# Meta-token state of gated linear attention in full 128-row matmuls, and its first head pair as one chain beside two projections

## The chip, the cores and the metric

The kernel runs on one core of one Trainium2 chip. A core has a matmul engine (TensorE, PE in the profile; PEld is its weight load), two elementwise engines (VectorE, DVE; ScalarE, ACT), GpSimd (POOL), and queues that start transfers (SP's and POOL's here). Each engine works through its own instructions in order and waits on semaphores for the others. The metric is the time of one execution in device microseconds; a kernel's time is the median of its runs.

## The reference

One decoder layer on 512 tokens and 16 learned meta tokens put ahead of them, width 1024. A normed input `u` goes through one wide projection, whose columns feed two branches: a retention branch (4 heads) and a gated linear attention (GLA, 4 heads, keys of 128, values of 256). Both are gated, projected, merged, projected once more and added to the input. The part around the change is GLA:

```python
log_a = log_sigmoid(glr @ w_gate_up + b_gate) / 16.0        # forget gate, per token, head and key channel
b = cumsum(ac, axis=2); b_last = b[:, :, -1]                 # inside a chunk
q_dec, k_inv, k_end = qc * exp(b), kc * exp(-b), kc * exp(b_last[:, :, None] - b)
intra = einsum(where(mask, einsum(q_dec, k_inv), 0), vc)
def step(state, xs):                                         # over chunks
    inter = einsum('bihd,bhde->bihe', q_n, state)
    state = state * exp(a_n)[..., None] + einsum('bjhd,bjhe->bhde', k_n, v_n)
    return state, inter
```

The meta tokens come first, so what they leave behind is the state with which the first token block begins: the sum over 16 rows of decayed keys times values.

## The kernel before

**Numbers.** Everything is float32. A large projection splits each operand into a rounded half (`hi`, type fp32r) and the rest (`lo`) and runs three fp32r matmuls in place of one (hi·hi, hi·lo, lo·hi). ACT casts the `hi` part and DVE subtracts the `lo` part (`split`, L163). Small products of the attention run in plain f32; the trace shows such a matmul as two instructions ("x2").

**Projections.** `quad` multiplies two column blocks of 256 by both halves of the tokens and of the contraction as a two-by-two block product with seven products in place of eight. Each product is 24 matmuls (L327). Two of its operands are weight sums that POOL's queue adds while it loads (L291); the results leave through `copy` (ACT), `put` and `evac` (DVE mostly). Between its products `quad` yields. In its `wide` form two pairs of PSUM banks serve in turn: the first product's bank is copied by ACT before the third product adds into it, and the second product's bank must have been read before the fourth overwrites it.

**Order.** The program is a set of Python generators. `weave(dense, chain, skip)` takes one step of a projection, then one of a chain, and so on, and lets the rest of the chain run out at the end. That order is the priority; the framework's planner then lays each engine's queue out by planned ready times, so a matmul of a projection may be put between matmuls of a chain. `pin` keeps the products of projections in their order, `after` keeps two instructions of one engine in a given order, `act` and `vec` do so for a list.

**GLA.** Heads go in two pairs, p = 0 and p = 1. `gla_attention(p)` is the chain: per block of 128 tokens `decays` (cumulated logs by matmul: tiles `ge` and `gf`, L933 to L937; exponentials on ACT into `gX`; scaled keys and queries `gK` and `gQ` on DVE, L946 and L947), `scores` (`gc`, L957 to L961) and `values` (`go` and `gsu`, L1006 to L1010, then a norm whose power is on POOL, L1022, and a scaling on ACT, L1025). Ahead of block 0 the meta tokens' state is made: `meta_state` (`gm`, L976 and L977), `meta_state2` (a transpose, `gmt`, L987), `meta_state3` (`gs`, L995). These take operands of 16 rows or 16 columns: `gsm`, `lah` and `lal`, `gkm`, `gkmt`, `gvm`. The logs of a block are split into `lah` and `lal`, one buffer each. After block 3's decays ACT applies eight Silus (L1051) to the gate `sg`.

For p = 0 the gate's projection `gla_g(0)` (tile `gg`, seven products) is woven with the first six steps of the attention; the other four steps follow; then the next pair's query and key projection `gla_qk(1)` (`gqk`) is woven with `gla_output(0)` (gating, L1071, and transposes `got`, L1078); then the value projection `gla_v(1)` alone. For p = 1 the attention is woven with `gla_g(1)` and the projections that follow it.

```python
    weave(gla_g(0), gla_attention(0), skip=1)
    weave(gla_qk(1), gla_output(0))
    drain(gla_v(1))
```

Query and key tiles `gq` and `gk` have one buffer each, which both pairs use. The chain's PSUM tiles share four banks (`pat`), those of the projections another four (`ppt`).

Of the kernel before, what the change touches and what calls it, by code (L numbers as in the profile page):

```python
# [21 lines left out]
F32 = mybir.dt.float32  # L22
F32R = mybir.dt.float32r
I32 = mybir.dt.int32
AF = mybir.ActivationFunctionType
# [3 lines left out]
P = 128  # L29
D = 1024  # L30
T = 512
NM = 16
TT = T + NM
HT = TT // 2
# [3 lines left out]
NTB = T // P  # L38
# [14 lines left out]
def constants():  # L53
    c = {}
    pos = np.concatenate([np.arange(NM, NM + 256), np.arange(HM),
                          np.arange(NM + 256, TT), np.arange(HM, NM)]).astype(np.float32)
    half = P
    inv = (10000.0 ** (-np.arange(half) / half)).astype(np.float32)
    ang = (pos[None, :] * inv[:, None].astype(np.float32)).astype(np.float32)
    c["rope"] = np.stack([np.cos(ang), np.sin(ang)], axis=1).astype(np.float32)  # L60

    j = np.arange(P)[:, None]
    cc = np.arange(T)[None, :]
    jm = np.arange(NM)[:, None]
# [24 lines left out]
    mm = np.arange(NM)  # L89
    c["gsum_meta"] = ((mm[:, None] > mm[None, :]) / 16.0).astype(np.float32)  # L90

    jj, ii = np.arange(P)[:, None], np.arange(P)[None, :]
    mA = (jj < 64) & (ii >= 64)
    mB = (jj // 64 == ii // 64) & (jj % 64 < 32) & (ii % 64 >= 32)
    mD = (jj // 32 == ii // 32) & (jj <= ii)
    c["gmask"] = np.stack([mA, mB, mD], axis=1).astype(np.int32)

    sel = np.zeros((P, P), np.float32)
    for g in range(4):
        for r in range(4):  # L100
# [9 lines left out]
def hybrid_kernel(ctx: ExitStack, tc: tile.TileContext, I, out: bass.AP):  # L110
    nc = tc.nc
# [50 lines left out]
    def split(hi, lo, src):  # L162
        return nc.scalar.copy(hi, src), nc.vector.tensor_sub(lo, src, hi.bitcast(F32))  # L163
# [10 lines left out]
    def act(ins):  # L174
        return queue("act", ins)
# [56 lines left out]
    def run(*gens):  # L232
        for g in gens:
            yield from g
# [284 lines left out]
    g1 = gctx.enter_context(tc.tile_pool(name="g1", bufs=1))  # L519
    la = g1.tile([P, 5, 512], F32, name="la")  # L520
    gsum = g1.tile([P, 640], F32R, name="gsum")
    gsm = g1.tile([NM, NM], F32R, name="gsm")
    gmask = g1.tile([P, 3, P], I32, name="gmask")
    gvm = [g1.tile([NM, 512], F32, tag="gvm", name=f"gvm{p}") for p in range(2)]
    gv = [g1.tile([P, NTB, 512], F32, tag="gv", name=f"gv{p}") for p in range(2)]
    gv0 = gv[0]

# [62 lines left out]

    def meta_v(psm, p):
        ps = meta_rows(psm, f"gvm{p}")
        nc.scalar.activation(gvm[p], ps[:NM], AF.Copy, scale=rt[:NM, NTB:])

    pss = [ppt(f"gv0_p{t}") for t in range(NTB)]
    casts = []
# [124 lines left out]
    for x in pmw:  # L721
# [14 lines left out]

    raws = (gsum[:, :512], xc.tile([P, 2, 256], F32, tag="xc", name="gs_raw").rearrange("p a b -> p (a b)"),
            I["gsum"][:, :512]), (gsum[:, 512:], laf[:, 2304:2432], I["gsum"][:, 512:]), \
        (gsm, fa[:NM, 1809:1809 + NM], I["gsum_meta"])
    for dst, raw, src in raws:  # L740
        nc.sync.dma_start(raw, src)
        nc.gpsimd.tensor_copy(dst, raw)
# [6 lines left out]
    def forget_gates():  # L749
# [9 lines left out]
                vec(nc.vector.scalar_tensor_tensor(g[32:64], pr[32:64, s, c0:c1], onec[32:64],  # L759
                                                   g[32:64].bitcast(F32), op0=ALU.add, op1=ALU.subtract))  # L760
        act(nc.scalar.copy(wzs, wz))
        act(nc.scalar.activation(gvm[0], gvs[:NM], AF.Copy, scale=rt[:NM, NTB:]))
        vec(nc.vector.tensor_sub(wzs[64:96], wz[64:96], wzs[64:96].bitcast(F32)))
        yield

# [62 lines left out]
        for b in (0, 4, 1, 2, 3):  # L828
            act(nc.scalar.activation(es[b], es[b], AF.Ln, bias=one))
            vec(nc.vector.tensor_sub(la[:, b, :], la[:, b, :], es[b]))  # L830
            if b == 4:

                parts["la"] = [gp.tile([P, 256], F32R, tag=f"la{x}", name=f"la{x}00") for x in "hl"]
                qsplit(*parts["la"], la[:, 0, :256])
        values(1)

# [16 lines left out]
                                     scale=(rt, rneg)[n][:, 2 * th + i:2 * th + i + 1])  # L853
        return f

    stb = []
    cnt = [0]
    G = {}

# [17 lines left out]
        yield from products  # L877

    def gla_qk(p):
        q = gp.tile([P, 2, T], F32, tag="gq", name=f"gq{p}")  # L880
        k = gp.tile([P, 2, 2, HT], F32, tag="gk", name=f"gk{p}")
        G["q", p], G["k", p] = q, k

        def evac_q(ps):
            for t in range(2):
                vec(nc.vector.tensor_mul(q[:, t, :].rearrange("p (h c) -> p h c", h=2),
                                         ps[t].rearrange("p (h c) -> p h c", h=2), rb[:, :, :256]))

        def evac_k(th, ps):
            for t in range(2):  # L890
                vec(nc.vector.tensor_mul(k[:, t, th, :], ps[t], rb[:, th, :]))

        def evac(n, th, x, y):
            d, w = (q[:, :, th * 256:(th + 1) * 256], 256) if n else (k[:, :, th, :], HT)
            if y is None:
                for t in range(2):
                    nc.vector.scalar_tensor_tensor(d[:, t], x[t][:, :w], (1.0, -1.0)[n], rb[:, th, :w],
                                                   op0=ALU.mult, op1=ALU.mult)
                return
            for t in range(2):  # L900
                nc.vector.tensor_add(d[:, t], x[t][:, :w], y[:, t, :w])
            nc.vector.scalar_tensor_tensor(d, d, (1.0, -1.0)[n], rb[:, th, :w].unsqueeze(1).to_broadcast([P, 2, w]),
                                           op0=ALU.mult, op1=ALU.mult)

        if p:
            yield from quad((C_GK + p * 256, C_GQ + p * 256), False, f"gqk{p}", evac, wide=True)
            return
        yield from proj_a(C_GQ + p * 256, False, f"gq{p}", evac_q)
        yield from proj_a(C_GK + p * 256, True, f"gk{p}", evac_k)

    def gla_attention(p):
# [3 lines left out]
        S = [None, None]  # L915
        Q, K, TO = {}, {}, {}

        def split_la(b, rows):
            if p == b == 0:
                return parts.pop("la")  # L920
            lh = gp.tile([P, 256], F32R, tag="lah", name=f"lah{p}{b}")
            ll = gp.tile([P, 256], F32R, tag="lal", name=f"lal{p}{b}")
            split(lh[:rows], ll[:rows], la[:rows, b, p * 256:(p + 1) * 256])
            return lh, ll

        def decays(b):
            lah, lal = split_la(b, P)
            for h in range(2):
                n = f"{p}{b}{h}"
                hc = h * P  # L930
# [38 lines left out]
                    nc.scalar.copy(KT[b, h], pc[:, 3 * P:])  # L969

        def meta_state():
            lah, lal = split_la(4, NM)
            for h in range(2):
                hc = h * P
                pm = pat(f"gm{p}{h}")
                nc.tensor.matmul(pm[:, :NM], lah[:NM, hc:hc + P], gsm, start=True, stop=False)  # L976
                nc.tensor.matmul(pm[:, :NM], lal[:NM, hc:hc + P], gsm, start=False, stop=True)  # L977
                km = gp.tile([P, NM], F32, tag="gkm", name=f"gkm{p}{h}", bufs=2)
                nc.scalar.activation(km, pm[:, :NM], AF.Exp)
                km2 = km.rearrange("p (h m) -> p h m", h=2)  # L980
                nc.vector.tensor_mul(km2, km2, k[:, h, :, 256:HT])
                S[h] = km

        def meta_state2():
            for h in range(2):
                pt = pat(f"gmt{p}{h}")
                nc.tensor.transpose(pt[:NM, :P], S[h], ident)  # L987
                kmt = gp.tile([P, P], F32, tag="gkt", name=f"gkmt{p}{h}", bufs=3)[:NM]
                nc.scalar.copy(kmt, pt[:NM, :P])
                S[h] = kmt  # L990

        def meta_state3():
# [48 lines left out]
        yield  # L1041
        values(1)
        scores(2)
        yield
        decays(3)

        sg = G["sg", p]
# [163 lines left out]
    for i in range(4):  # L1211
        stb.append(gp.tile([P, P], F32, name=f"stb{i}"))
        nc.gpsimd.memset(stb[i], 0.0)
    weave(gla_g(0), gla_attention(0), skip=1)
    weave(gla_qk(1), gla_output(0))
    drain(gla_v(1))
    weave(run(gla_g(1), gates_first(), gla_branch()), run(gla_attention(1), gla_sums()))
    gctx.close()
# [430 lines left out]
```

## Time and profile before

| | |
|---|---|
| runs shown | 751.65, 751.62, 750.5 us; median 751.62 us |
| the profiled execution | 750.33 us |
| its span, first to last instruction | 748.6 us |
| PE busy | 738.6 us |
| DVE busy | 607.7 us |
| ACT busy | 450.3 us |
| POOL busy | 137.5 us |
| granted PE clock, mean | 0.999 |

The profiled execution's time is its span and 1.73 us around it. Matmuls overlap in the records (one is some 0.28 us long while the next starts 0.11 us behind it), so PE's busy share doesn't say how densely it works; the chain of waits, which gives to each instruction only the time by which it moved the end, does. The stretch that the change touches runs from 58 us (first `gg` product) to 124 us (last `gqk` product), and for the second head pair from 146 us to 182 us.

### The profile page before, as it was taken

Reading aid. Unit: us, or ns where it says so; the run is one execution under the profiler, and the core shown is the slowest. Engines: PE = TensorE matmul, PEld = TensorE weight load, DVE = VectorE, ACT = ScalarE, POOL = GpSimd, SP = SyncE. Lnnn points to the kernel's source line nnn. Section 1 sums busy time; section 2 is a strip of 40 time slices with the busy share of each in tenths; the row PEclk is TensorE's granted clock in tenths of the full one; section 3 lists DMA queues with packets and bytes.
Section 4 is the critical chain, followed back from the end, with each engine's and each line's share of the span. In section 5 each row is a group of like instructions: output and inputs, shape, how many; then the busy total and the mean of one; then the engine's idle time right before and its main releaser. Section 6 shows DMA issues by size and latency. Waiting matters only on the chain.

```text
span 748.6 us, 14064 instructions
## 1 busy us (share of the span) xinstructions
PE 738.6 (99%) x5595; PEld 691.7 (92%) x5595; DVE 607.7 (81%) x873; ACT 450.3 (60%) x764; POOL 137.5 (18%) x172
## 2 busy tenths in 40 slices
PE   9999999999999999999999999999999999999996
PEld 6799899989999999999989999989999989988996
DVE  6699877679897799888957688967697989775995
ACT  7898584666975466546546555646555656532562
POOL 2111110101221122110520100540011210111142
PEclk9999999999999999999999999999999999999999
DMA  9873521821589972734783652796476356687503
GB/s 298 278 162 77 121 62 53 198 85 58 129 187 280 305 169 87 170 113 141 200 250 115 133 149 96 199 213 163 126 169 136 113 141 197 227 195 206 133 29 113
DMA packets 100138, 117.42 MB, mean 157 GB/s; under 512 B 5732, under 2 KB 90852, under 8 KB 99816
## 3 DMA queue, kind: packets, MB, share of 16 engines
q1 hardware_dynamic: 79896, 88.19, 37.1%
q0 software_dynamic: 19888, 27.79, 20.4%
q8 instruction: 44, 0.72, 0.4%
q10 hardware_dynamic: 288, 0.53, 0.2%
q14 instruction: 22, 0.18, 0.1%
HBM read 104.44 MB, written 11.53 MB: 155 GB/s over the span
## 4 chain that ended last, share of the span: by engine, by line
PE 89%; DVE 7%; issue 2%; ACT 1%; POOL 0%; POOLq 0%; DVEq 0%; ACTq 0%
PE rqk_b L327 6%; PE rv_b L327 6%; PE rg_b L327 5%; PE rqk_c L327 5%; PE br_p L201 4%; PE br_p L202 4%; PE br_p L198 4%; PE gg_b L327 3%; PE mg_b L327 3%; PE mr_b L327 3%; PE gv_p L652 3%; PE rv_c L327 3%; PE bg_b L327 2%; PE rg_c L327 2%; PE gk_p L437 2%
## 5 line engine op out<-in xcount | busy, mean ns | idle before, releaser
L202 PE MATMUL br_p<-oh,br_l 128*128 128x512 f32 x128 | 49.9, 390 | 0.0
L201 PE MATMUL br_p<-ol,br_h 128*128 128x512 f32 x128 | 49.9, 390 | 0.0
L198 PE MATMUL br_p<-oh,br_h 128*128 128x512 f32 x128 | 49.8, 389 | 0.0
L163 ACT CAST rv_h<-rv_w 128x1024 fp32r<-128x1024 f32 x24 | 25.3, 1053 | 25.3 <-DVE rv_w L381 10.4
L327 PE MATMUL rqk_b<-xh,rqk_h 128*128 128x264 f32 (+1 forms) x128 | 36.2, 283 | 0.0
L327 PE MATMUL rqk_b<-xh,rqk_l 128*128 128x264 f32 (+1 forms) x128 | 36.1, 282 | 0.0
L327 PE MATMUL rqk_b<-xl,rqk_h 128*128 128x264 f32 (+1 forms) x128 | 36.0, 281 | 0.0
L327 PE MATMUL rv_b<-rv_l,xh 128*128 128x256 f32 x128 | 35.5, 277 | 0.5 <-DVE rv_l L163 0.5
L163 DVE TENSOR_TENSOR rv_l<-rv_w,rv_h 128x1024 fp32r<-128x1024 f32 x24 | 29.3, 1221 | 8.1 <-ACT rv_h L163 8.1
L327 PE MATMUL rv_b<-rv_h,xh 128*128 128x256 f32 x128 | 35.8, 280 | 0.0
L327 PE MATMUL rv_b<-rv_h,xl 128*128 128x256 f32 x128 | 35.4, 277 | 0.0
L327 PE MATMUL rg_b<-rg_h,xh 128*128 128x256 f32 x128 | 35.4, 277 | 0.0
L327 PE MATMUL rg_b<-rg_h,xl 128*128 128x256 f32 x128 | 35.4, 276 | 0.0
L327 PE MATMUL rg_b<-rg_l,xh 128*128 128x256 f32 x128 | 35.4, 276 | 0.0
L163 DVE TENSOR_TENSOR rg_l<-rg_w,rg_h 128x1024 fp32r<-128x1024 f32 x20 | 24.4, 1220 | 8.1 <-ACT rg_h L163 8.1
L163 ACT CAST rg_h<-rg_w 128x1024 fp32r<-128x1024 f32 x20 | 21.0, 1052 | 15.6 <-PE br_p L201 5.9
L291 POOL DMA_DIRECT2D rqk_x<-in_w_in_dram x8 | 10.4, 1302 | 102.2 <-PE rv_b L327 64.2
L202 PEld LDWEIGHTS br_p<-oh,br_l 128*128 128x128 f32 x128 | 24.0, 188 | 5.0
L1380 ACT ACTIVATE on<-av,nm,g_r 128x512 f32<-128x512 f32 x16 | 12.5, 779 | 26.4 <-DVE nm L1378 26.4
L198 PEld LDWEIGHTS br_p<-oh,br_h 128*128 128x128 f32 x128 | 24.0, 188 | 4.6
L201 PEld LDWEIGHTS br_p<-ol,br_h 128*128 128x128 f32 x128 | 24.0, 188 | 4.5
L163 ACT CAST rqk_h<-rqk_w 128x1024 fp32r<-128x1024 f32 x20 | 21.0, 1052 | 11.8 <-PE rqk_c L327 2.9
(624 smaller groups left out, 3155.4 us busy)
## 6 DMA issues: line engine op xcount, KB each, us to landing
rv_w<-in_w_in_dram SPq DMA_DIRECT2D x16, 512.0 KB, 4.2
br_w<-in_w_branch_ret_dram SPq DMA_DIRECT2D x16, 512.0 KB, 3.4
rqk_w<-in_w_in_dram SPq DMA_DIRECT2D x12, 512.0 KB, 5.0
rg_w<-in_w_in_dram SPq DMA_DIRECT2D x12, 512.0 KB, 4.9
rqk_x<-in_w_in_dram SPq DMA_DIRECT2D x8, 512.0 KB, 4.6
rqk_x<-in_w_in_dram POOLq DMA_DIRECT2D x8, 512.0 KB, 7.9
rg_x<-in_w_in_dram SPq DMA_DIRECT2D x8, 512.0 KB, 3.6
rg_x<-in_w_in_dram POOLq DMA_DIRECT2D x8, 512.0 KB, 7.6
```

The lines of the kernel that those rows point to most:

```text
L163: return nc.scalar.copy(hi, src), nc.vector.tensor_sub(lo, src, hi.bitcast(F32))
L198: m = nc.tensor.matmul(o, lh, rh, start=first, stop=False)
L201: nc.tensor.matmul(o, lh, rl, start=False, stop=False)
L202: m = nc.tensor.matmul(o, ll, rh, start=False, stop=last)
L291: x = nc.gpsimd.dma_start(t, block(0, 1), accum_op=ALU.add)
L327: m = nc.tensor.matmul(ps[t][:, :n] if wide else ps[t], l, r, start=first and j == 0, stop=kk == 3 and j == 2, skip_group_check=not fresh ...
L437: m = nc.tensor.matmul(pss[t][th], l[:, kk, c], r, start=first and j == 0, stop=kh == 1 and kk == 3 and j == 2, skip_group_check=not meta ...
L652: m = nc.tensor.matmul(pss[t], (al if j == 1 else ah)[t // 2, kh][:, k, c], (lo if j == 2 else hi)[:, kk, :], start=q == kk == j == 0, sto ...
L1380: nc.scalar.activation(on, ps, AF.Identity, scale=r, bias=nm)
```

## The change

Five edits.

- The constant `gsum_meta` is padded from 16 to 128 rows of zeros; `gsm`, `gvm` and the split of the meta block's logs have 128 rows; the decayed meta keys lie in the first 16 columns of two zeroed 128 x 128 tiles `kms`, used by both head pairs. So `gm`, `gmt` and `gs` are matmuls with 128 rows and 128 weight columns.
- `lah` and `lal` have two buffers.
- For p = 0 one yield goes: `values(1)`, `scores(2)`, `decays(3)` and the Silus are one step.
- `gla_output(0)` follows the attention in one chain, and `gla_qk(1)` follows `gla_g(0)` in one row of projections; the two are woven.
- `gla_qk(1)` takes its `gq` and `gk` tiles only after its first product, when the chain step with `decays(3)` has been written down.

```diff
-    c["gsum_meta"] = ((mm[:, None] > mm[None, :]) / 16.0).astype(np.float32)
+    c["gsum_meta"] = np.concatenate([(mm[:, None] > mm[None, :]) / 16.0, np.zeros((P - NM, NM))]).astype(np.float32)
...
-    gsm = g1.tile([NM, NM], F32R, name="gsm")
+    gsm = g1.tile([P, NM], F32R, name="gsm")
...
-    gvm = [g1.tile([NM, 512], F32, tag="gvm", name=f"gvm{p}") for p in range(2)]
+    gvm = [g1.tile([P, 512], F32, tag="gvm", name=f"gvm{p}") for p in range(2)]
...
-        nc.scalar.activation(gvm[p], ps[:NM], AF.Copy, scale=rt[:NM, NTB:])
+        nc.scalar.activation(gvm[p], ps, AF.Copy, scale=rt[:, NTB:])
...
-        (gsm, fa[:NM, 1809:1809 + NM], I["gsum_meta"])
+        (gsm, fa[:, 1809:1809 + NM], I["gsum_meta"])
...
         if p:
-            yield from quad((C_GK + p * 256, C_GQ + p * 256), False, f"gqk{p}", evac, wide=True)
+            products = quad((C_GK + p * 256, C_GQ + p * 256), False, f"gqk{p}", evac, wide=True)
+            next(products)
+            yield
+            q, k = tiles()
+            yield from products
             return
...
-            lh = gp.tile([P, 256], F32R, tag="lah", name=f"lah{p}{b}")
-            ll = gp.tile([P, 256], F32R, tag="lal", name=f"lal{p}{b}")
-            split(lh[:rows], ll[:rows], la[:rows, b, p * 256:(p + 1) * 256])
+            lh = gp.tile([P, 256], F32R, tag="lah", name=f"lah{p}{b}", bufs=2)
+            ll = gp.tile([P, 256], F32R, tag="lal", name=f"lal{p}{b}", bufs=2)
+            split(lh, ll, la[:, b, p * 256:(p + 1) * 256])
...
-                nc.tensor.matmul(pm[:, :NM], lah[:NM, hc:hc + P], gsm, start=True, stop=False)
-                nc.tensor.matmul(pm[:, :NM], lal[:NM, hc:hc + P], gsm, start=False, stop=True)
-                km = gp.tile([P, NM], F32, tag="gkm", name=f"gkm{p}{h}", bufs=2)
-                nc.scalar.activation(km, pm[:, :NM], AF.Exp)
-                km2 = km.rearrange("p (h m) -> p h m", h=2)
+                nc.tensor.matmul(pm[:, :NM], lah[:, hc:hc + P], gsm, start=True, stop=False)
+                nc.tensor.matmul(pm[:, :NM], lal[:, hc:hc + P], gsm, start=False, stop=True)
+                nc.scalar.activation(kms[h][:, :NM], pm[:, :NM], AF.Exp)
+                km2 = kms[h][:, :NM].rearrange("p (h m) -> p h m", h=2)
                 nc.vector.tensor_mul(km2, km2, k[:, h, :, 256:HT])
-                S[h] = km
...
-                nc.tensor.transpose(pt[:NM, :P], S[h], ident)
-                kmt = gp.tile([P, P], F32, tag="gkt", name=f"gkmt{p}{h}", bufs=3)[:NM]
-                nc.scalar.copy(kmt, pt[:NM, :P])
+                nc.tensor.transpose(pt[:, :P], kms[h], ident)
+                kmt = gp.tile([P, P], F32, tag="gkt", name=f"gkmt{p}{h}", bufs=3)
+                nc.scalar.copy(kmt, pt[:, :P])
...
         scores(2)
-        yield
+        if p:
+            yield
         decays(3)
...
-    weave(gla_g(0), gla_attention(0), skip=1)
-    weave(gla_qk(1), gla_output(0))
+    for h in range(2):
+        kms.append(gp.tile([P, P], F32, name=f"gkm{h}"))
+        nc.gpsimd.memset(kms[h], 0.0)
+    weave(run(gla_g(0), gla_qk(1)), run(gla_attention(0), gla_output(0)), skip=1)
```

More of the change, by code (lines that the diff above doesn't have):

```diff
@@ L761, in forget_gates @@
         act(nc.scalar.copy(wzs, wz))
-        act(nc.scalar.activation(gvm[0], gvs[:NM], AF.Copy, scale=rt[:NM, NTB:]))
+        act(nc.scalar.activation(gvm[0], gvs, AF.Copy, scale=rt[:, NTB:]))
         vec(nc.vector.tensor_sub(wzs[64:96], wz[64:96], wzs[64:96].bitcast(F32)))
@@ L831, in forget_gates @@
             if b == 4:
-                parts["la"] = [gp.tile([P, 256], F32R, tag=f"la{x}", name=f"la{x}00") for x in "hl"]
+                parts["la"] = [gp.tile([P, 256], F32R, tag=f"la{x}", name=f"la{x}00", bufs=2) for x in "hl"]
                 qsplit(*parts["la"], la[:, 0, :256])
@@ L854, in rows_into @@
         return f
-    stb = []
+    stb, kms = [], []
     cnt = [0]
@@ L879, in gla_qk, with tiles @@
     def gla_qk(p):
-        q = gp.tile([P, 2, T], F32, tag="gq", name=f"gq{p}")
-        k = gp.tile([P, 2, 2, HT], F32, tag="gk", name=f"gk{p}")
-        G["q", p], G["k", p] = q, k
+        def tiles():
+            q = gp.tile([P, 2, T], F32, tag="gq", name=f"gq{p}")
+            k = gp.tile([P, 2, 2, HT], F32, tag="gk", name=f"gk{p}")
+            G["q", p], G["k", p] = q, k
+            return q, k
         def evac_q(ps):
@@ L905, in gla_qk @@
         if p:
-            yield from quad((C_GK + p * 256, C_GQ + p * 256), False, f"gqk{p}", evac, wide=True)
+            products = quad((C_GK + p * 256, C_GQ + p * 256), False, f"gqk{p}", evac, wide=True)
[3 more added lines that the diff above has]
+            yield from products
             return
+        q, k = tiles()
         yield from proj_a(C_GQ + p * 256, False, f"gq{p}", evac_q)
@@ L916, in gla_attention, with split_la @@
         Q, K, TO = {}, {}, {}
-        def split_la(b, rows):
+        def split_la(b):
             if p == b == 0:
                 return parts.pop("la")
-            lh = gp.tile([P, 256], F32R, tag="lah", name=f"lah{p}{b}")
-            ll = gp.tile([P, 256], F32R, tag="lal", name=f"lal{p}{b}")
-            split(lh[:rows], ll[:rows], la[:rows, b, p * 256:(p + 1) * 256])
+            lh = gp.tile([P, 256], F32R, tag="lah", name=f"lah{p}{b}", bufs=2)
+            ll = gp.tile([P, 256], F32R, tag="lal", name=f"lal{p}{b}", bufs=2)
+            split(lh, ll, la[:, b, p * 256:(p + 1) * 256])
             return lh, ll
         def decays(b):
-            lah, lal = split_la(b, P)
+            lah, lal = split_la(b)
             for h in range(2):
@@ L971, in meta_state @@
         def meta_state():
-            lah, lal = split_la(4, NM)
+            lah, lal = split_la(4)
             for h in range(2):
```

## The prediction

> **What bounds the kernel now.** First the page: the span, and the chain that ended last, by engine.
>
> ```profile
> span 748.6 us, 14064 instructions
> ...
> PE 89%; DVE 7%; issue 2%; ACT 1%; POOL 0%; POOLq 0%; DVEq 0%; ACTq 0%
> ```
>
> PE carries 89% of the chain, so a microsecond taken from PE's stream is a microsecond of the kernel unless something else is late there. PE's busy share can't say how densely it works, since records overlap. So I went next to busy time by stretch, from the first `gg` product to the last `gqk` product.
>
> ```profile
> core 0: us, PE busy (x) PEld busy (x) DVE busy (x) ACT busy (x) POOL busy (x), PEclk, DMA share, GB/s
> ...
> 64.00:70.00 6.00, 5.99 (x46) 5.44 (x45) 5.86 (x11) 5.65 (x15) 1.69 (x3) 1.00 0.28 87
> ...
> 90.00:97.00 7.00, 6.54 (x39) 5.76 (x39) 6.39 (x15) 5.42 (x17) 1.40 (x4) 1.00 0.04 7
> ```
>
> Only 90 to 97 us shows PE idle, 7.00 - 6.54 = 0.46 us. From 64 to 70 us DVE is nearly full (5.86 of 6.00): a second bound to keep in mind. Transfers are light there (a DMA share of 0.28 and 0.04) and the granted clock is 1.00. What is left to win is thus the price of single matmuls. The chain of waits, in order of time, gives it (start, us by which the piece moved the end, what).
>
> ```profile
> 67.84 0.31 PE gm L976 x2
> 68.16 0.32 PE gg_c L327
> 68.48 0.22 PE gc L957 x2
> ...
> 68.92 0.31 PE gm L977 x2
> 69.23 0.42 PE gc L959 x2
> ...
> 70.43 0.11 PE gc L961
> ...
> 73.17 0.22 PE gmt L987 x2
> 73.39 2.75 PE gg_b L327 x24
> ...
> 78.38 0.62 PE gs L995 x2
> 79.00 0.67 PE gg_c L327 x4
> 79.68 0.62 PE gs L995 x2
> 80.30 1.72 PE gg_c L327 x13
> ...
> 83.22 0.43 PE gsu L1010 x2
> ```
>
> A `gg` matmul costs 2.75 / 24 = 0.115 us in a run of its own kind, but the first one behind `gm` cost 0.32. The pair of `gs` with 16 rows cost 0.62; the pair of `gsu`, the same 256 columns with 128 rows, 0.43. So matmuls of 16 rows cost more than full ones, and so does what stands behind them. The second head pair shows the same:
>
> ```profile
> 152.50 0.23 ACT lah L163
> ...
> 152.77 0.38 PE gm L976 x2
> 153.16 2.36 PE gg_b L327 x19
> 155.52 0.31 PE gm L977 x2
> 155.83 0.79 PE gg_b L327 x5
> ...
> 162.89 0.62 PE gs L995 x2
> 163.51 0.66 PE gg_b L327 x4
> 164.18 0.62 PE gs L995 x2
> 164.80 2.14 PE gg_b L327 x17
> ```
>
> **Part 1: 128 rows.** Sums go by the chain's pieces.
>
> `gm`, first pair: the four matmuls cost 0.31 + 0.31; the matmul behind the first two cost 0.32 - 0.115 = 0.21 too much, the two behind the others 0.42 - 0.22 = 0.20. Together 1.03 us. Second pair: 0.38 + 0.31, then 2.36 - 19 x 0.115 = 0.18 and 0.79 - 5 x 0.115 = 0.22: 1.09 us. Afterwards four fp32r matmuls of 128 rows and 16 columns stand there, a form that the trace doesn't have. At most each costs what `gg` with 256 columns does, 0.115; a cost below zero is excluded, since it still is an instruction with a weight load. I take 0.08, nearer to the record of 128 columns (0.11 for `gc`) than to zero: 0.32 for four. Gain 0.71 and 0.77, with bounds of 0.57 to 1.03 and 0.63 to 1.09.
>
> The Trainium skill ("TensorE: Matmul & The Clock Gate", section "Back-to-back issue gap") puts an issue floor of about 25 ns under matmuls of 1 to 64 columns; by it the four would cost 0.10 and each gain would be 0.22 larger. No run so far shows it.
>
> `gs`, first pair: 0.62 + 0.62, then 0.67 - 4 x 0.115 = 0.21 and 1.72 - 13 x 0.115 = 0.23: 1.68. Afterwards it has `gsu`'s form, 0.43 for each pair of records: 0.86. Gain 0.82. Second pair: 1.24 + 0.20 + 0.19 = 1.63, gain 0.77.
>
> The transposes `gmt` cost 0.22 for two; full ones (`gc` L961) 0.11 each. Nothing.
>
> Rows together: 0.71 + 0.77 + 0.82 + 0.77 = 3.07 us, bounds 2.8 to 3.7.
>
> The same page of the Trainium skill (section "Why this matters for your kernels") says that one matmul with 32 contracted rows takes as long as one with 128, and recommends packing several small ones. By that, padding would win nothing here. The rows above disagree (0.62 against 0.43); it comes back as a rival.
>
> What the padding adds off PE: two zero fills on POOL and a wider cast of `gsm`.
>
> ```profile
> L1213 POOL MEMSET stb<- 128x128 f32 x4 | 0.6, 198 | 0.0
> ...
> L742 POOL CAST gsm<-fg_a 16x16 fp32r<-16x16 f32 x1 | 0.2, 186 | 0.0
> ```
>
> ```profile
> 17.95 0.34 POOL L588 CAST sel<-la 128x128 fp32r<-128x128 f32 x1 [13.45 <-DMA la<-in_sel_dram]
> ...
> 78.53 1.30 POOL L291 DMA_DIRECT2D gqk_x<-in_w_in_dram  x1 [8.31 <-ACT gX L939]
> ```
>
> The fills have the form of `stb`'s, 2 x 0.198 = 0.4 us; POOL then idles 13.45 us before the cast of `sel`, which hides them. Without that cover they cost 0.4. The cast goes from 0.186 to less than the 0.34 of `sel`'s eight times as many columns, and `gm` reads the result only at 67.84. The constant's transfer carries 112 more rows of 64 bytes, with the same one issue on SP. ACT's and DVE's steps on 128 in place of 16 rows keep their row length. All nothing.
>
> **Part 2: one chain beside two projections.** The stall that it can remove: its two ends in the chain of waits, then PE's own record of the second.
>
> ```profile
> 92.47 0.02 issue
> ...
> 95.34 0.45 PE gf L936
> ```
>
> ```profile
> 95.34 0.45 PE L936 MATMUL gf<-gsum,lah 128*128 128x384 f32 x1 [0.46 <-ACT gon L1025]
> ```
>
> `gf` of block 3 needs a PSUM bank that `go` of block 1 holds until its norm (ACT, DVE, POOL, ACT again) is through. From 92.47 to 95.34 the end waits 2.87 us for that. In this time PE did `scores(2)`, six pairs of `gc` at 0.22 and two transposes at 0.11 (1.54 us), and one pair of `ge`, 256 columns as `gg` has (0.23). So PE lost at most 2.87 - 1.54 - 0.23 = 1.10 us, and at least the idle 0.46. Now a whole `gqk` product (24 matmuls as in `gg`'s, some 2.75 us) stands ahead of that step and the next one is ready, with five more to put between the later steps. The planner already pulls single `gqk` matmuls into such gaps, so something of this is lost again where PE's fixed order and ACT's real times disagree. I take 0.8 us, between 0 and 1.10. Less than zero is the slower rival's.
>
> Passed queues: the transfers of `gqk` were issued long before (POOL's second weight sum at 78.53, above), ahead of the steps that move, so neither SP's nor POOL's order changes there. The norm's POOL power keeps its place in the chain. Waits that are added: the second product's evacuation on DVE writes `gk`, which must wait for block 3's `gK` and `gQ`; behind it in DVE's order are only later evacuations and splits, and PE needs that bank at the fourth product.
>
> **Part 3: two buffers for the logs.** The one place where the chain shows the split is the second pair's 152.50: 0.23 us in which PE waits for ACT's cast, which stands behind the exponentials. A second buffer lets it go first: 0 to 0.23 (nothing below, since the later split of a block has no other user to delay), I take 0.1.
>
> **Taken back.** After 67.8 us DVE may not follow. `gg_l` for the fifth product was made at 71.57 and used at 73.35:
>
> ```profile
> 71.57 1.22 DVE L163 TENSOR_TENSOR gg_l<-gg_x,gg_h 128x1024 fp32r<-128x1024 f32 x1
> ```
>
> ```profile
> 73.35 0.28 PE L327 MATMUL gg_b<-gg_l,xh 128*128 128x256 f32 x1
> ```
>
> It ended at 72.79, 0.56 us ahead of its use; PE comes 0.71 earlier, so 0.15 us is lost there, up to 0.5 if the rest of `gm`'s bound is won as well. I take 0.2.
>
> **Sum.** 3.07 + 0.8 + 0.1 - 0.2 = 3.8 us less. Against the profiled execution (750.33 us, span 748.6): 746.5, span 744.8. The median of the runs shown is 1.29 above the profiled execution; there it makes 751.62 - 3.8 = 747.8 us. Nothing behind the changed part takes it back: PE leads the chain there too, and the second pair's steps all start earlier by the same time.
>
> **Rivals.**
>
> *The ACT block comes between the products (slower).* ACT loads a table and runs eight Silus behind block 3's exponentials:
>
> ```profile
> 98.02 1.28 ACT L1051 ACT_TABLE_LOAD   x1
> ...
> 102.28 0.49 ACT L1051 ACTIVATE gsg<-gsg,rneg 128x256 f32<-128x256 f32 x1
> ...
> 103.39 0.36 ACT L340 COPY gqk_x<-gqk_b 128x264 f32<-128x264 f32 x1
> 106.31 1.09 ACT L163 CAST gqk_h<-gqk_x 128x1024 fp32r<-128x1024 f32 x1
> ```
>
> That is 4.75 us, and here the copies of the first `gqk` bank already come after it. The third product adds into that bank and so waits for two copies (0.72); with one cast (1.09) behind the block, 6.6 us of ACT stand before it, and if the chain's own PE steps are stuck behind ACT too, only the second product (2.75) covers. A wait of 3.8, and 1.1 for the next cast: 4.9. Then part 2 gives nothing and 751.6 - 3.07 - 0.1 + 0.2 + 4.9 = 753.5 us. It turns slower from a wait of 3 us on. For it: the copy at 103.39 stands right behind the Silus now. Against: the first bank is now full before block 3's exponentials, where ACT has 7.00 - 5.42 = 1.58 us free, so its copies should go first; and `values(2)` and `scores(3)` need only what stands ahead of the Silus.
>
> *DVE is the bound of the first stretch.* Then the first pair's 1.53 us of rows ends in waits for `lo` parts, and half of part 2 with them: 3.8 - 1.53 - 0.4 = 1.9 less if all else holds, 749.7; with the second pair's `gm` (0.77) lost too, 750.5. For it: 5.86 of 6.00. Against: 6.39 of 7.00 later, and 0.56 us of slack at the split above.
>
> *Rows are not the price.* If the extra is that of a change between fp32r and plain f32, padding wins nothing, and parts 2 and 3 alone remain: 750.7 us. Against it: `gc` is f32 behind fp32r at 68.48 and costs its 0.22; `gm` is fp32r ahead of fp32r at 152.77, and the `gg` behind it still pays. This is also what the Trainium skill's rule on 32 rows (same page and section as above) would make of the time.
>
> *The projection was in the gaps anyway,* so part 2 is nothing: 748.6. This lies inside the forecast's range.
>
> **How the numbers follow.** The forecast (3.8 less, with bounds from 2.8 - 0.5 = 2.3 to 3.7 + 1.1 + 0.2 = 5.0, part 2 at nothing included): 0.70. DVE bound: 0.11. Rows not the price: 0.06. ACT block: 0.08. Another shift of the later plan, either way: 0.05. A measurement of this kernel tells no less than about 0.2%, 1.5 us, from no change. Faster by more: the forecast, a third of the DVE case, half the last: 0.76. Within: the rest of the DVE case, rows not the price, a little of the others: 0.15. Slower: the ACT case and a little: 0.09. The range runs from 751.6 - 5.0 - 0.9 = 745.7 (0.9 for the spread of 1.15 us among the runs shown) to 750.7, where rival three lies; the ACT case and outliers stay outside.
>
> **What would show it.** In the profile after: `gm` and `gs` as 128-row forms, `gs` pairs at 0.43 in the chain and no matmul far above 0.115 behind them; no ACT or POOL piece in the chain between the last `gg` and the first `gqk` product; the last `gqk` product ending some 2 us earlier, `gla_g(1)`'s last some 3.5 us earlier, and that lead kept to the end. It is wrong if `gs` keeps 0.62, if DVE pieces appear in the chain before 90 us, or if `gqk` waits for ACT copies.

## The result and the profile after

The changed kernel takes 749.2 us (median of 12 runs, 748.46 to 750.24), the kernel before beside it 751.0 us (12 runs, 749.9 to 752.43): a ratio of 0.9976 with a 95% interval of 0.9968 to 0.9984. That is 1.8 us less, where 3.8 were forecast. A second timing gave 749.31 against 750.95 us, 0.9977 (0.9968 to 0.9986); one of its 15 runs of the kernel before, 811.63 us at a granted clock of 0.851, was in a slow state and is left out of that ratio (the median without it is 750.85). The profiled execution took 748.96 us, with a span of 747.2.

First the page of the changed kernel: the span and the chain that ended last, by engine.

```profile
span 747.2 us, 14063 instructions
...
PE 83%; DVE 9%; issue 3%; DMA 2%; ACT 2%; POOL 0%; POOLq 0%; DVEq 0%; ACTq 0%
```

PE's share of the chain fell from 89% to 83%, DVE's rose from 7% to 9% and DMA's from 0 to 2%: the end now goes through transfers and elementwise steps in places where PE led before. Busy time by stretch (PE, PEld, DVE, ACT, POOL, granted clock, DMA share, GB/s):

```profile
64.00:70.00 6.00, 5.86 (x51) 5.63 (x50) 6.00 (x11) 5.88 (x15) 4.05 (x3) 1.00 0.28 87
90.00:97.00 7.00, 6.07 (x43) 5.56 (x41) 6.73 (x15) 4.46 (x12) 0.69 (x1) 1.00 0.42 128
```

PE idles 0.93 us between 90 and 97 us, where before it idled 0.46: the stall that the new order was to remove has grown. DVE is full from 64 to 70 us. Then the chain of waits through the first pair:

```profile
64.52 0.14 issue
64.67 0.25 PE gm L983
64.91 0.11 PE gm L984
65.03 2.73 PE gg_b L327 x23
67.76 0.01 PE gm L983
67.77 0.11 PE gm L984
67.88 0.22 PE gg_c L327
...
77.93 0.54 PE gs L1000 x2
78.47 0.48 PE gg_c L327 x4
78.95 0.58 PE gs L1000 x2
79.53 1.16 PE gg_c L327 x10
```

`gs` costs 0.54 and 0.58 where it cost 0.62, and the products behind it nothing extra any more: 0.48 for four and 1.16 for ten are the 0.115 each of a run of their own kind. The first `gm` comes 3 us earlier, and the end is moved by 0.14 us of "issue" just ahead of it. The chain names no releaser. ACT's exponential `gX` ended 0.10 us before (64.30 + 0.27), so a wait for the PSUM bank that it read is likely, but not shown.

Where a part of the extra cost of 16 rows sat can be read from the records of the weight load, before and after:

```profile
78.31 0.29 PEld L995 LDWEIGHTS gs<-gvm,gkmt 16*128 16x128 f32 x2 [0.25 <-ACT gX L940]
78.93 0.19 PEld L327 LDWEIGHTS gg_c<-gg_l,xh 128*128 128x128 f32 x1 [0.33 <-issue]
```

```profile
77.77 0.30 PEld L1000 LDWEIGHTS gs<-gvm,gkmt 128*128 128x128 f32 x2
78.10 0.19 PEld L327 LDWEIGHTS gg_c<-gg_l,xh 128*128 128x128 f32 x1
```

Behind the 16-row `gs` the next weight load began only 0.33 us after the last had ended, together with its own matmul (78.94). Behind the 128-row `gs` it begins 0.03 us after.

Where the time went shows best as a lead. I matched each matmul of two traces with itself and took the difference of the starts, the median in each stretch, less what the traces differ by before any edited code (45 to 58 us: between -0.53 and +0.60 us from execution to execution, already there behind the warm-up matmuls). In us ahead of the kernel before; a minus is behind. The last column is what the `bg` stage takes (221-227 less 235-250).

| kernel | 78-90 | 124-130 | 157-165 | 172-180 | 221-227 | 235-250 | end | lost at `bg` |
|---|---|---|---|---|---|---|---|---|
| changed | 0.89 | 1.10 | 1.85 | 1.65 | 1.79 | 1.00 | 0.93 | 0.79 |
| changed, second profile | 0.89 | 1.09 | 1.84 | 1.05 | 1.18 | 1.15 | 1.09 | 0.03 |
| rows only | 1.17 | 1.17 | 1.52 | 0.89 | 0.89 | -0.21 | -0.22 | 1.10 |
| order only | -0.02 | 0.19 | 0.17 | 0.17 | 0.18 | -0.03 | 0.01 | 0.21 |
| buffers only | -0.01 | -2.49 | -2.02 | -2.18 | -2.07 | -3.24 | -3.29 | 1.17 |
| rows and order | 1.16 | 1.37 | 1.71 | 1.76 | 1.74 | 0.29 | 0.19 | 1.45 |
| second product first | 0.89 | 2.28 | 3.05 | 2.81 | 2.92 | 2.23 | 2.21 | 0.69 |
| `mr` sum later | 0.89 | 1.10 | 1.85 | 2.34 | 2.34 | 0.83 | 0.79 | 1.51 |
| `og` transfer first | 0.89 | 1.10 | 1.85 | 1.28 | 1.40 | 1.39 | 0.87 | 0.01 |
| both of these | 0.87 | 1.05 | 1.80 | 2.29 | 2.29 | 2.19 | 2.17 | 0.10 |
| all three | 0.85 | 2.24 | 3.02 | 3.53 | 3.51 | 3.41 | 3.34 | 0.10 |
| all three, one buffer | 1.15 | 2.54 | 2.91 | 3.31 | 3.41 | 3.41 | 3.36 | 0.00 |

The profiled executions of the changed kernel and of before differ by 0.93 us at the end and by 0.43 in the start, 1.37 us in their times; the medians by 1.8, since the profiled execution of before was a good one (750.33 against its median of 751.0). All leads are against this one execution, so a part of what a kernel seems to lose may be its good luck: its transfer into `og` (below) took 8.2 us, the shortest of the nine profiles that issue it in that order (8.2 to 9.4).

The lead grows to 1.10 us behind the last `gqk` product and to 2.37 just ahead of the second pair's `go` (the row for 164.96 us in the match). Then it is lost in two places. The first is DVE's queue at 160 us, and PE's wait for it:

```profile
160.56 1.23 DVE L364 TENSOR_TENSOR mr_x<-mr_w,mr_w 128x1024 f32<-128x1024 f32 x1 [1.85 <-issue]
...
164.11 0.75 DVE L1002 COPY gS<-gs 128x256 f32<-128x256 f32 x2
```

```profile
164.58 0.70 PE L1011 MATMUL go<-gS,gQ 128*128 128x256 f32 x2 [0.41 <-DVE gS L1002]
```

A weight sum of the `mr` projection waits 1.85 us for its transfer, with the second pair's `gK`, `gQ` and `gS` behind it. It waited as long before (1.90), but PE came later. In the two profiles of the changed kernel this place takes 0.72 and 1.32 us of the 2.37, and the 0.60 between them is the difference of that one transfer (4.4 and 5.0 us). The second is the `bg` stage, in the chain of waits:

```profile
208.43 5.80 DMA bg_x<-in_w_branch_gla_dram
...
214.87 0.80 POOL bg_x L291
215.68 8.29 DMA og<-og1gq
...
224.15 1.07 ACT gs L1157
...
225.24 1.24 DVE gs L1158
...
226.52 5.50 PE bg_b L327 x44
```

A load, the accumulating load behind it on POOL's queue, a transfer into `og` that POOL issues only then, an ACT and a DVE step: PE waits for the last of them.

### The profile page after: what moved, and what is told of

It reads as the page before. It is cut to its first block, busy times and chain, and to the rows that moved or that the text cites. A ratio compares the mean times of both kernels' runs of the same rounds, so it can differ in the third digit from the quotient of the medians.

```text
span 747.2 us, 14063 instructions
## 1 busy us (share of the span) xinstructions
PE 735.6 (98%) x5595; PEld 691.4 (93%) x5595; DVE 607.2 (81%) x873; ACT 450.0 (60%) x764; POOL 140.7 (19%) x174
## 4 chain that ended last, share of the span: by engine, by line
PE 83%; DVE 9%; issue 3%; DMA 2%; ACT 2%; POOL 0%; POOLq 0%; DVEq 0%; ACTq 0%
PE rqk_b L327 6%; PE rv_b L327 6%; PE rg_b L327 5%; PE rqk_c L327 5%; PE br_p L202 4%; PE br_p L201 4%; PE br_p L198 4%; PE gv_p L652 3%; PE mg_b L327 3%; PE rv_c L327 3%; PE rg_c L327 2%; PE mr_b L327 2%; PE gg_b L327 2%; PE bg_b L327 2%; PE gk_p L437 2%
```

## The experiments

All times stand beside the kernel before on the same chip. The ratio and its interval are those of the record and can differ a little from the quotient of the medians. For rows alone, order alone, buffers alone and the second product first, before took 751.0 us (27 runs).

**Rows alone.** Before with the 128-row meta state (the edits to `gsum_meta`, `gsm`, `gvm` and `kms`), in the old order and with one buffer for the logs.

```diff
-                km = gp.tile([P, NM], F32, tag="gkm", name=f"gkm{p}{h}", bufs=2)
+                nc.scalar.activation(kms[h][:, :NM], pm[:, :NM], AF.Exp)
```

> Before with the 128-row meta state alone. Theory A (rows carry the whole gain; the rest of the change gives nothing): 1.5 to 2.0 us faster than before, pairs of gs at 0.54 to 0.58 in the chain in place of 0.62, nothing extra on the gg matmuls behind them. Rival B (the rows' gain of 1.7 us on PE is eaten by waits in both pairs and the woven order carries what is left): under 0.8 us faster.

Measured: 749.77 us, 0.9983 (0.9974 to 0.9992). That is 1.2 us less, between the theory's 1.5 and the rival's 0.8. Its chain of waits through the first pair:

```profile
68.31 0.12 PE gm L976 x2
68.43 0.22 PE gg_c L327
...
69.09 0.12 PE gm L977 x2
69.22 0.32 PE gc L959 x2
...
78.27 0.47 PE gs L993 x2
78.73 0.47 PE gg_c L327 x4
79.20 0.59 PE gs L993 x2
79.79 1.50 PE gg_c L327 x13
```

`gm`: 0.12 + 0.12, and 0.10 too much in each of the pieces behind it: 0.44 in place of 1.03. `gs`: 0.47 + 0.59 and nothing behind: 1.06 in place of 1.68. Together 1.21 us, and the lead table has 1.17. The rows are a price, then: the same matmuls with the same columns got cheaper, and so did what follows them. The second pair wins 0.94 (from 1.17 to 2.11 at 164.96 us). In this execution, the slowest of its 11 (751.04 us), that and more is lost at the `go` wait and in the `bg` stage. (The Trainium skill, "TensorE: Matmul & The Clock Gate", section "Why this matters for your kernels", has a matmul of 32 contracted rows take as long as one of 128; here the pair of 16 rows took 0.62 and that of 128 rows 0.47 to 0.59, and 0.2 less behind it. The measurement decides.)

**Order alone.** The woven chain, the missing yield and the later tiles; 16 rows and one buffer.

```diff
-    weave(gla_g(0), gla_attention(0), skip=1)
-    weave(gla_qk(1), gla_output(0))
+    weave(run(gla_g(0), gla_qk(1)), run(gla_attention(0), gla_output(0)), skip=1)
```

> Before with the woven order alone (attention and output of the first pair as one chain beside gg and gqk, one yield fewer). Theory A: no difference within 0.5 us; gf of block 3 still waits for the bank that go of block 1 holds, PE idle there 0.5 to 1.0 us. Rival B: 0.8 to 1.2 us faster, no idle there.

Measured: 750.39 us, 0.9994 (0.9985 to 1.0003). The lead behind the last `gqk` product is 0.19 us and is gone behind `bg`. PE's stretch around the old stall is emptier than before (3.54 busy of 4.00 there):

```profile
94.00:98.00 4.00, 3.07 (x23) 2.74 (x22) 3.61 (x10) 1.89 (x8) 0.70 (x1) 1.00 0.72 219
```

**Buffers alone.** Before with `bufs=2` on the split logarithms.

```diff
-            lh = gp.tile([P, 256], F32R, tag="lah", name=f"lah{p}{b}")
+            lh = gp.tile([P, 256], F32R, tag="lah", name=f"lah{p}{b}", bufs=2)
```

> Before with two buffers for the split logarithms alone. Theory A: no difference within 0.4 us; gm stands earlier in PE's order and waits about 0.3 us for a PSUM bank that an exponential on ACT still reads. Rival B: 0.2 to 0.5 us faster through the second pair's cast.

Measured: 751.81 us, 1.0010 (1.0002 to 1.0019): slower by 0.8 us. The profiled execution, at 753.36 us the slowest of its 11, shows how the loss grows. POOL's power in the norm took twice its 0.80 us, PE stood, and then ran at half speed (PE's record, POOL's, and busy time by stretch):

```profile
95.93 0.39 PE L933 MATMUL ge<-gsum,lah 128*128 128x256 f32 x1 [1.69 <-ACT gon L1025]
```

```profile
93.40 1.60 POOL L1022 TENSOR_TENSOR gss<-gss,mhalf 128x2 f32<-128x2 f32 x1 [2.49 <-DVE gss L1021]
```

```profile
94.00:98.00 4.00, 2.31 (x16) 1.95 (x14) 2.20 (x9) 2.08 (x7) 1.19 (x2) 0.93 0.45 131
98.00:101.00 3.00, 3.00 (x11) 2.59 (x10) 2.42 (x4) 2.46 (x7) 0.36 (x1) 0.52 0.01 3
```

The granted clock is 0.52 from 98 to 101 us, behind an idle of 1.69 us. The median lost less than this execution, so not every one has it. What the median's 0.8 us are made of isn't settled; the 0.44 us that are lost at the first `gm` (64 to 70 us) are made up by 84.

**Rows and order, one buffer.** The changed kernel without `bufs=2`. For this, the `mr` sum later, the `og` transfer first and all three with two buffers, before took 751.25 us (16 runs).

```diff
-            lh = gp.tile([P, 256], F32R, tag="lah", name=f"lah{p}{b}", bufs=2)
+            lh = gp.tile([P, 256], F32R, tag="lah", name=f"lah{p}{b}")
```

> The changed kernel with one buffer for the split logarithms, as before: rows and order alone. Theory from the run with two buffers alone (0.8 us slower than before): the second buffer lets the first pair's `gm` move ahead to where its PSUM bank is still being read, and PE waits there 0.3 us; without it that wait goes and the kernel is 0.3 to 0.8 us faster than the changed one: about 748.7. Rival: what the two buffers cost alone came from a stall of PE at 94 to 96 us and the lower granted clock (0.52) behind it, which the woven order does not have; then one buffer or two make no difference here (749.2), or one is slower by the 0.23 us that the second pair's cast waited before (749.4).

Measured: 749.73 us, 0.9974 (0.9963 to 0.9985), where the changed kernel has 0.9976: no difference. The profile has both halves: 0.27 more lead at 78 to 90 us without the second buffer, 0.14 less at 157 to 165. The rival's "no difference" held. Its reason, that alone the buffers hurt through the stall at 94 us and the slower clock behind it, is shown by one execution only.

**Second product first.** The changed kernel, with `gqk`'s second product ahead of block 3's decays in the order.

```diff
             next(products)
             yield
+            next(products)
+            yield
             q, k = tiles()
+            next(products)
...
-        if p:
-            yield
+        yield
         decays(3)
```

(`quad` yields once more, ahead of the first write to the tiles.)

> The changed kernel, but with gqk's second product ahead of block 3's decays on PE (a yield more in the projection before its second bank is read, and the attention's yield back). Theory A (the stall at gf is a wait for the PSUM bank of go, which the planner put too early, and nothing else): idle at gf gone, last gqk product 0.8 to 1.2 us earlier than in the changed kernel, 0.5 to 1.0 us faster than it, 2.3 to 2.8 us faster than before. Rival C (PE waits there for ACT's general lateness): the wait moves to the next gqk product, no difference from the changed kernel.

Measured: 748.13 us, 0.9964 (0.9952 to 0.9977). PE's idle time at the old stall is gone (3.07 busy of 4.00 in the changed kernel):

```profile
94.00:98.00 4.00, 4.00 (x36) 3.97 (x35) 2.75 (x10) 1.96 (x8) 0.69 (x1) 1.00 0.87 250
```

The lead behind the last `gqk` product is 2.28 us, 1.18 more than in the changed kernel. So the gain was there, at the place named, and the change didn't fetch it. In the changed kernel PE's record shows why:

```profile
95.75 0.28 PE L941 MATMUL ge<-gsum,lal 128*128 128x256 f32 x1
96.96 0.45 PE L943 MATMUL gf<-gsum,lah 128*128 128x384 f32 x1 [0.93 <-ACT gon L1030]
97.25 0.33 PE L944 MATMUL gf<-gsum,lal 128*128 128x384 f32 x1
97.42 0.28 PE L327 MATMUL gqk_c<-xh,gqk_h 128*128 128x264 f32 x1
```

The first `gqk` product ran ahead of block 1's `go`, so the norm that frees the bank came later too (ACT's `gon` at 96.07, before 94.45), and the second product was queued behind the waiting `gf`. Some 0.4 us of it is DVE's: the norm's `gss` could start when ACT was through at 94.68, but stood behind two `gS` until 95.10.

**`mr` sum later.** The changed kernel, with the waiting weight sum ordered behind `gQ` of block 1.

```diff
-            nc.vector.tensor_add(x3, w22, w12)
+            s = nc.vector.tensor_add(x3, w22, w12)
+            if add_after is not None:
+                after(s, add_after)
```

> The changed kernel, with one of DVE's weight sums (`mr_x`, which waited 1.85 us for its transfer at 160.56 in the changed kernel's profile, with the second pair's gK, gQ and gS of block 1 queued behind it) ordered behind gQ of block 1. Theory: this queueing is what made `go` of block 1 late and cost PE 0.57 us at 164.58; without it the last `mr` product ends 0.4 to 0.6 us earlier. The total follows only as far as the transfer into `og` behind it allows: 0 to 0.5 us faster than the changed kernel, 748.7 to 749.2. Rival: the sum made later delays the first `mr` product in turn, and the last `mr` product ends where it did or later: 749.2 to 749.7.

Measured: 748.29 us, 0.9954 (0.9936 to 0.9971). The `go` wait is gone: PE's record of the same `go` has no idle time,

```profile
165.03 0.59 PE L1013 MATMUL go<-gS,gQ 128*128 128x256 f32 x2
```

and the lead is 2.34 us, where the changed kernel has 1.65 and 1.05. The median lies below the expected 748.7 to 749.2. In the profiled execution, the slowest of its six (750.14 us), the `bg` stage took 1.51 of the lead back, with the longest transfer seen:

```profile
og<-og1gq POOLq DMA_DIRECT2D x1, 512.0 KB, 9.4
```

**`og` transfer first.** The changed kernel, with POOL's issue of the transfer into `og` ahead of the accumulating load of the second `bg` block (called the weight sum in the expectation).

```diff
+                    if t is x3 and behind3 is not None:
+                        after(x, behind3)
...
-        nc.gpsimd.dma_start(a00, a01, accum_op=ALU.add)
+        G["og"] = nc.gpsimd.dma_start(a00, a01, accum_op=ALU.add)
```

> The changed kernel, with one swap in POOL's order: the accumulating transfer into `og` (issued at 215.68 us in the changed kernel's profile, behind the weight sum of the second `bg` block, which itself waited until 214.87 for a load) is issued ahead of that sum. PE, DVE and ACT keep their orders. Theory: this transfer (8.29 us) and the ACT and DVE steps behind it set when `bg_b` at 226.52 can start, so whatever the first stretch wins beyond that point is lost there (PE lost 0.7 us to it). Then the issue moves to about 214, the wait of 0.7 us goes, and the kernel is 0.4 to 0.9 us faster than the changed one: about 748.5. Rival: the transfer waits for its own source instead (the same queue or the same producer), is issued as late as now or takes longer beside the load it passes, or the sum that is now later holds up the `bg` product: no difference (749.2) or slower (749.8).

Measured: 748.98 us, 0.9960 (0.9945 to 0.9975): not told apart from the changed kernel. The `bg` stage took nothing (0.01), as expected, but in this execution the `go` wait had already taken 1.11 (a lead of 2.39 became 1.28, with 0.79 of idle time at that `go`), and at 282 us 0.5 went in the next projection.

**Both of these.** For this, the changed kernel again and all three with one buffer, before took 750.95 us (15 runs).

```diff
+        yield from quad((C_MR, C_MR + 256), False, "mr0", evac, adds=False, add_after=G["gQ", 1, 1])
...
+                            behind3=G["og"] if j else None)
```

> The changed kernel with the `mr` weight sum behind gQ of block 1 and the transfer into `og` ahead of the second `bg` block's accumulating load, without the edit of the `gqk` order. Theory: the 2.3 us of lead that the first of the two edits showed ahead of the `bg` stage is kept through it, so the kernel ends 1.2 to 1.6 us ahead of the changed one, at a ratio of about 0.9957 to before. Rival: the loads and transfers of the `bg` stage cap the lead at about 1.4 us whatever their order (so far the `og` edit alone kept 1.4 behind `bg`): ratio 0.997.

Measured: 748.24 us, 0.9966 (0.9953 to 0.9978), against 749.31 of the changed kernel beside it: 1.07 us. The expected 0.9957 lies inside the interval and so does the rival's 0.997; the profile speaks for the first, since 2.19 of 2.29 us of lead pass the stage. That both edits are needed rests on the profiles: by their ratios one alone (0.9954, 0.9960) and both (0.9966) aren't told apart. Its DMA view has the two transfers that changed places:

```profile
og<-og1gq POOLq DMA_DIRECT2D x1, 512.0 KB, 6.0
...
bg_x<-in_w_branch_gla_dram POOLq DMA_DIRECT2D x1, 512.0 KB, 9.3
```

The transfer into `og` took 5.5 to 6.5 us in the four profiles that issue it first, and 8.2 to 9.4 in the nine that issue it behind the load; PE waits for this one alone.

**The changed kernel again.** The same instructions, beside these.

> The changed kernel once more, every instruction the same, timed beside the kernels that follow. Theory: 1.8 us under the kernel before, as the first time (ratio 0.9976). In its profile the lead over before behind the last `gqk` product is 1.1 us less the difference at the start, and the `bg` stage takes back between 0.2 and 1.5 us of it, by how long the transfer into `og` (8.2 to 9.4 us in the profiles so far) happens to take; if the lead at the end is 0.9 us whatever this transfer takes, that reading falls.

Measured: 749.31 us, 0.9977 (0.9968 to 0.9986). Here the `bg` stage took only 0.03, where the `go` wait had already taken 1.32 of the lead (PE idled 1.01 us there). In these two executions what the first place leaves, the second takes, and the lead at the end is 0.93 and 1.09. My reading that the transfer's length alone decides falls for this pair (8.3 us in both): what counts is the lead with which PE arrives, too. But the loss doesn't need a lead. The kernel with the buffers alone arrives 2.07 us behind and loses 1.17 more, of which 0.9 is its longer transfer (9.1 us against 8.2 before); in rows only the transfer took 9.0 us (a loss of 1.10), in rows and order 9.2 (1.45), in `mr` sum later 9.4 (1.51), so there too most of the loss is its length.

**All three, with two buffers and with one.** The last two edits and the `gqk` order together; then the same without `bufs=2`.

> The changed kernel with all three edits: the second `gqk` product ahead of block 3's decays (1.1 us faster than the changed kernel by itself), the transfer into `og` ahead of the second `bg` block's weight sum, and the `mr` weight sum behind gQ of block 1. Theory: with the transfer issued earlier, the lead that the first stretch wins is kept to the end: the first edit's lead of 3.4 us at the end of the `mr` products (it kept 2.65 behind `bg`) then shows in full, 747.0 to 747.6, and with the `mr` edit 746.7 to 747.4. Rival: behind `bg` another transfer or DVE step is late by as much, and it ends at the first edit's 748.1.

> All three edits, with one buffer for the split logarithms in place of two. Theory: the second buffer costs 0.3 us ahead of 70 us (PE waits for the bank of the first `gm`) and wins about 0.3 at 150 to 165 us, so no difference: 0.9938 of before, as with two. Rival: with the later losses mended the 0.8 us that the second buffer cost alone show: 0.993 or less. Other rival: the second pair's cast waits again and it is 0.3 us slower, 0.9942.

Measured: 747.11 us, 0.9938 (0.9922 to 0.9953), and 746.73 us, 0.9946 (0.9934 to 0.9959). The lead is kept from 157 us to the end, 3.34 and 3.36 us. One buffer or two is no difference. This is 2.1 us under the changed kernel's 749.2 and 2.6 under the 749.31 that was measured beside the second. It is also about what the forecast had promised for the change, by coincidence: two of the three edits are at places that the forecast took at nothing.

## Why the prediction was right in direction and wrong in size

The direction, the range and the place of the first gain held; half of the size was missing. Of the 3.8 us forecast, the lead at 165 us shows 2.37: 2.11 by rows, 0.19 by order, the rest with the buffers. By the forecast's own steps:

- **Part 1, `gs` and `gm` (3.07).** Right mechanism, mis-sized. First pair 1.17 in place of 1.53, second 0.94 in place of 1.54, by rows alone: 2.11, below the lower bound of 2.8. This term was too big by 0.96, more than any other. "Afterwards it has `gsu`'s form, 0.43 for each pair" failed: `gs` took 0.47 to 0.59. That `gs` stands behind fp32r matmuls isn't the reason, since a pair of `go` right behind fp32r `gg_b` costs 0.43 in the same trace (81.03). What differs is the weight load: in the changed kernel that of `gs` starts with its matmul (78.83 both; the pair costs 0.58), that of `go` 0.11 us ahead (80.76 and 80.87); in rows alone that of the first `gs` starts 0.07 ahead (78.03 and 78.10), and the pair costs 0.47. Why it starts late stays open. The `gm` matmuls came out at 0.06 each, below the 0.08 taken, but the piece behind each pair still pays 0.10, taken at zero. The floor of 25 ns for `gm` (the Trainium skill, "TensorE: Matmul & The Clock Gate", section "Back-to-back issue gap") wasn't reached; the same row has about 62 ns per matmul with hardware decode off, which the 0.06 would fit, but no run here shows which of the two holds.
- **Part 2, one chain (0.8).** The step that failed is "Now a whole `gqk` product (24 matmuls as in `gg`'s, some 2.75 us) stands ahead of that step and the next one is ready". It stood ahead of the step that frees the bank as well, and the next one was put behind the wait. Order alone won 0.19. The stall was real: with the second product moved it gave 1.18 more. The mechanism was right, the placing was not read. The bound of 1.10 was wrong twice: PE's `gsu` ran until 92.72, 0.25 us into the wait, which leaves 0.85; and with the second product moved the order wins 1.39 from the row 78-90 to 124-130 (0.89 to 2.28), so more than this stall was to be had there. What the rest is, isn't settled.
- **Part 3, buffers (0.1).** The step "nothing below, since the later split of a block has no other user to delay" failed. The freed split let `gm` come 3 us earlier, to a place where PE loses time (0.33 behind at 64 to 70 us). With the rest of the change it ends at no difference; alone it costs 0.8.
- **Taken back, DVE at the fifth split (0.2).** Not seen: the first pair's lead in rows alone (1.17) is that of its pieces (1.21). DVE did bind, but at 160 us.
- **"Nothing behind the changed part takes it back."** This step failed too. Of 2.37 us of lead at 165 us, 0.93 and 1.09 reached the end of the two profiles, and 1.8 by the medians. So it cost between 0.6 and 1.4 us; the profiles can't say it closer, since that of before was 0.7 us under its median. With both places mended the kernel gained 1.07. A `mr` weight sum that waits for its transfer (4.4 and 5.0 us in the two profiles) and the chain into `bg` had no slack before, and PE's lead doesn't make a transfer shorter. In the trace of before the slack could have been read: DVE's `gs` ended at 226.77 + 1.21 = 227.98, and PE's `bg_b` started at 228.02.

```profile
226.77 1.21 DVE L1152 SCALAR_TENSOR_TENSOR gs<-og,gs 128x1024 fp32r<-128x1024 f32 x1
```

Of the rivals, the ACT block did not come between the products: the first bank's copy stands at 90.62, ahead of the Silus.

```profile
90.62 0.45 ACT L340 COPY gqk_x<-gqk_b 128x264 f32<-128x264 f32 x1
...
99.34 1.28 ACT L1057 ACT_TABLE_LOAD   x1
```

DVE was the bound at 160 us and for a part of the stall at `gf`; in the first stretch the chain has no DVE piece ahead of 92 us. The DVE rival's time is nearest all the same (1.9 less, 749.7, where 1.8 less was measured), and that is luck: its step, that the first pair's rows end in waits for `lo` parts, did not happen. "Rows are not the price" fell with rows alone. "The projection was in the gaps anyway" (748.6) is nearly as close in time, for another reason: the gap was there and was missed.

## What to carry to other kernels

When PE gets faster in one stage, walk the chain behind it for places where a transfer or a queue on another engine ends just when PE arrives: "PE leads the chain" says who was last, not by how much. Price an instruction together with its weight load and the row behind it: here the same form cost 0.43 us where its weights were loaded ahead and up to 0.59 where the load began with the matmul. And work that is to cover a wait must be between the waiting instruction and the one that frees it, in the engine's own order, not only somewhere near it.

## What was not expected of the hardware

- A PE idle of 1.69 us was followed by a granted clock of 0.52 for some 3 us (the kernel with the buffers alone), while 0.93 us in the changed kernel left it at 1.00. The Trainium skill ("TensorE: Matmul & The Clock Gate", section "What's actually happening") has the clock halved after an idle window of about 3.4 us, free-running; here, in one execution, the clock fell behind an idle time of about half that.
- Of two accumulating transfers of 512 KB behind each other on POOL's queue the first took 6.0 us and the second 9.3, so their order is worth over 2 us to whoever waits for the first alone (5.5 to 6.5 us issued first, 8.2 to 9.4 issued second).
- The start of the kernel differs by over a microsecond between executions of nearly the same program (-0.53 to +0.60 against before, all of it in the first 8 us), as much as most of the edits here are worth. The first four `gv_p` matmuls behind the warm-up took 1.61 us in before, 1.16 in the changed kernel and 2.16 in `mr` sum later, the next four 1.08 to 1.10 in each; what sets this isn't settled.
